# Attention inputs in a hybrid layer: q's heads transposed in pairs and split behind the transpose, k doubled ahead of one transpose, the row maximum negated, q's norm product on POOL

## The chip, the cores and the metric

The kernel runs on one core of a Trainium2 chip. The metric is the device time of one execution in microseconds (us). Before the change three runs gave a median of 1288.86 us (1288.18 to 1288.86). The engines are PE (TensorE: matrix products and transposes, results in PSUM), DVE (VectorE), ACT (ScalarE), POOL (GpSimd, which here works on SBUF alone) and SP (SyncE, which issues all DMAs).

## The reference

One layer on 2048 positions of width 1024. A normalised input goes through one projection; half of its columns feed a gated DeltaNet scanned in both directions (4 heads of 128), the other half a windowed attention (8 query heads, 2 key/value heads, width 64). Both results are gated, joined and projected back. The change touches the attention alone:

```python
q = rotary(rms_norm(q.reshape(b, s, 8, 64), q_norm_w), cos, sin)
k = rotary(rms_norm(k.reshape(b, s, 2, 64), k_norm_w), cos, sin)
...
scores = jnp.einsum('bnqhgd,bnkhd->bnhgqk', qb, kb) * (SWA_HEAD_DIM ** -0.5)
scores = jnp.where(valid[None, :, None, None], scores, -jnp.inf)
mx = jnp.maximum(jnp.max(scores, axis=-1, keepdims=True), sink)
p = jnp.exp(scores - mx)
denom = jnp.sum(p, axis=-1, keepdims=True) + jnp.exp(sink - mx)
out = jnp.einsum('bnhgqk,bnkhd->bnqhgd', p / denom, vb)
```

Blocks of 128 queries see 384 keys: their own block and one on each side.

## The kernel before

All data is f32. Matrix products that need the full precision are made from parts in a rounded format (`F32R`): a value is split into a high part (a rounding copy, on ACT) and a low part (the value less the high part, on DVE), and the products of the parts are added in PSUM.

**Stages.** `phase_a` goes over the sequence in two halves of 8 chunks of 128 positions. In a half it first projects keys, values and queries by position (`seq_chunk`, stored in DRAM), then goes over the chunks `c`: `kv_chunk` and `q_chunk` prepare keys and queries one chunk ahead, `attend` does the attention of the chunk before, and between them stand the projections by feature, which carry most of PE's work: `conv_pair` (the DeltaNet's q, k, v with their convolution; tiles `pf_c` on PE, four `acc` additions on DVE for each, L241) and `gate_pairs` (`pf_z`, nearly PE alone). In the first half two groups of gates are mixed in ahead of and behind the convolutions; in the second half only the convolutions are, and the gates follow after the attention. `phase_b` then does the DeltaNet's matrices, inverses and scans and the output projections.

**What the change touches.** `rope` (L272) rotates and normalises: POOL makes the rotated rows `t1` (L276 to L279), ACT and DVE the sums of squares `rs`, POOL the power -1/2 (L284), DVE the product of `t1` and `rs` (L285). `q_chunk` takes two groups of four heads: ACT copies the group to the high part of `qd`, DVE makes the low part beside it (L321, L322), so each head has 128 columns, its high and its low 64. PE transposes each head into a PSUM tile `ptq` (L326), and ACT copies the four to `q2` (L327), whose rows 0 to 63 are then the high part and 64 to 127 the low one. `kv_chunk` does the same for a key head with the high part doubled (`kd`, two copies of 64 columns) and the low part doubled: four transposes a chunk (L308) and a copy to `k2` (L309). In `attend` two products a head (L343, L344) give the scores; one DVE instruction (L345) adds the mask and takes the row maximum, starting from the head's sink; another (L349) negates the maximum into `nm`, which ACT's exponential takes as its bias (L350). POOL multiplies the probabilities `pr` by the reciprocal sum (L359), PE transposes them (L364, PSUM tiles `pt`), ACT and DVE split them (`ph`, `pl`), and PE multiplies with the values.

**Buffers.** `ptq`, `ptk` and `pt` share a ring of two PSUM tiles (pool `pst`); the scores have two tiles of their own, the projections three, the output one.

**Order.** The order on each engine is not the order of the code. `set_order` collects all instructions, their dependencies and the rings of buffers, and a list scheduler with a cost for each instruction writes an order for every engine, which then holds. So an edit at one place can move instructions anywhere in the program.

Of the kernel before, what the change touches and what calls it, by code (L numbers as in the profile page):

```python
# [10 lines left out]
ALU = mybir.AluOpType  # L11
# [56 lines left out]
def phase_a(ctx, wide, tc, t, ident, nw, bd, gp, mix_sw, kq_d, v_d, zdn_d, zsw_d, q_pool):  # L68
# [24 lines left out]
    for a, src in ((qw, t["qw"]), (kw, t["kw"])):  # L93
        dma(a[:, 0], src.partition_broadcast(P))
        dma(a[:, 1, 0:32], src[32:64].partition_broadcast(P))
        dma(a[:, 1, 32:64], src[0:32].partition_broadcast(P))
    sink = const("sink", [P, NQ], t["sinks"].partition_broadcast(P))
    edge = const("edge", [P, 12, 4])
    half_neg = const("half_neg", [P, 16])
    V.memset(half_neg, -0.5)  # L100
    A.activation(cw, cw, AF.Copy, scale=0.5)
    A.activation(qw, qw, AF.Copy, scale=0.125)

    xhi, xlo = {}, {}

# [166 lines left out]
    def rope(src, n, tab, name):  # L272
        sv = src.rearrange("p (h d) -> p h d", d=64)
        t1 = sp.tile([P, 8, 64], F32, tag="t1", name=f"t1{name}")[:, :n]
        t2 = sp.tile([P, 8, 64], F32, tag="t2", name=f"t2{name}")[:, :n]
        G.tensor_tensor(t1, sv, tab[:, 0:1].to_broadcast([P, n, 64]), ALU.mult)  # L276
        G.tensor_tensor(t2[:, :, 0:32], sv[:, :, 32:64], tab[:, 1:2, 0:32].to_broadcast([P, n, 32]), ALU.mult)
        G.tensor_tensor(t2[:, :, 32:64], sv[:, :, 0:32], tab[:, 1:2, 32:64].to_broadcast([P, n, 32]), ALU.mult)
        G.tensor_tensor(t1, t1, t2, ALU.add)  # L279
        rs = sp.tile([P, 8], F32, tag="rsq", name=f"rs{name}")[:, :n]  # L280
        A.activation(t2, sv, AF.Square)
        V.tensor_reduce(rs, t2, axis=AX.X, op=ALU.add)
        G.tensor_scalar(rs, rs, 1.0 / 64, EPS, ALU.mult, ALU.add)
        G.tensor_tensor(rs, rs, half_neg[:, :n], ALU.pow)  # L284
        V.tensor_tensor(t1, t1, rs.unsqueeze(2).to_broadcast([P, n, 64]), ALU.mult)  # L285
        return t1

    def kv_chunk(c):
        sl = c % 4 + 2
        if c and c % 4 == 0:  # L290
            V.tensor_copy(k2[:, :, :, 0 : 2 * P], k2[:, :, :, 4 * P : 6 * P].bitcast(F32))
            V.tensor_copy(v2[:, 0:2], v2[:, 4:6].bitcast(F32))
        kv = sp.tile([P, 2 * P], F32, tag="kv", name=f"kv{c}")
        dma(kv, kv_d[c])
        kk = kv[:, 0:P]
        vv = kv[:, P : 2 * P].rearrange("p (h d) -> p h d", d=64)
        A.activation(v2[:, sl, :, 0:64], vv, AF.Copy)
        G.tensor_tensor(v2[:, sl, :, 64:128], vv, v2[:, sl, :, 0:64].bitcast(F32), ALU.subtract)
        kn = rope(kk, 2, rope_tab(c, kw, "k"), f"k{c}")
        kd = sp.tile([P, 512], F32R, tag="qd", name=f"kd{c}")  # L300
        kd = kd.rearrange("p (g s a d) -> p g s a d", g=2, s=2, a=2)
        knb = kn.unsqueeze(2).to_broadcast([P, 2, 2, 64])
        A.activation(kd[:, :, 0], knb, AF.Copy)
        V.tensor_tensor(kd[:, :, 1], knb, kd[:, :, 0].bitcast(F32), ALU.subtract)
        pt = pst.tile([P, 4, P], F32, tag="pst", name=f"ptk{c}")
        for g in range(2):
            for s in range(2):
                T.transpose(pt[:, 2 * g + s], kd[:, g, s].rearrange("p a d -> p (a d)").bitcast(F32), ident)  # L308
        A.activation(k2[:, :, :, sl * P : (sl + 1) * P], pt.rearrange("p (g s) n -> p g s n", g=2), AF.Copy)  # L309

    def q_chunk(c):
        qq = sp.tile([P, 512], F32, tag="qq", name=f"ql{c}")
        dma(qq, q_d[c])
        tab = rope_tab(c, qw, "q")
        r = []
        qa = rope(qq, 8, tab, f"q{c}")
        for g in range(2):
            qn = qa[:, 4 * g : 4 * g + 4]
            qd = sp.tile([P, 512], F32R, tag="qd", name=f"qd{c}_{g}")
            qd = qd.rearrange("p (h a d) -> p h a d", h=4, a=2)  # L320
            A.activation(qd[:, :, 0], qn, AF.Copy)  # L321
            V.tensor_tensor(qd[:, :, 1], qn, qd[:, :, 0].bitcast(F32), ALU.subtract)  # L322
            q2 = sp.tile([P, 4, P], F32R, tag="q2", name=f"q2_{c}_{g}", bufs=4)
            pt = pst.tile([P, 4, P], F32, tag="pst", name=f"ptq{c}_{g}")
            for j in range(4):
                T.transpose(pt[:, j], qd[:, j].rearrange("p a d -> p (a d)").bitcast(F32), ident)  # L326
            A.activation(q2, pt, AF.Copy)  # L327
            r.append(q2)
        return r

    def attend(c, q2):
        sl = 1 if c % 4 == 3 and c < NCH - 1 else c % 4 + 2
        lo, hi = (1 if c == 0 else 0), (2 if c == NCH - 1 else 3)
        n = (hi - lo) * P
        k0 = (sl - 1 + lo) * P
        for g in range(2):
            pr = [sp.tile([P, 3 * P], F32, tag="pr", name=f"pr{c}_{g}_{j}", bufs=6) for j in range(4)]
            st = sp.tile([P, 4, 4], F32, tag="st", name=f"st{c}_{g}")
            mx, nm, den, es = (st[:, i] for i in range(4))
            for j in range(4):  # L340
                hh = 4 * g + j
                ps = pss.tile([P, 3 * P], F32, tag="pss", name=f"s{c}_{hh}")
                T.matmul(ps[:, :n], q2[g][:, j], k2[:, g, 0, k0 : k0 + n], start=True, stop=False)  # L343
                T.matmul(ps[:, :n], q2[g][:, j], k2[:, g, 1, k0 : k0 + n], start=False, stop=True)  # L344
                V.tensor_tensor_reduce(  # L345
                    pr[j][:, :n], ps[:, :n], mask[:, lo * P : hi * P], 1.0, sink[:, hh : hh + 1],
                    ALU.add, ALU.max, accum_out=mx[:, j : j + 1],
                )
                V.tensor_scalar(nm[:, j : j + 1], mx[:, j : j + 1], -1.0, None, ALU.mult)  # L349
                A.activation(  # L350
                    pr[j][:, :n], pr[j][:, :n], AF.Exp, bias=nm[:, j : j + 1], accum_out=den[:, j : j + 1]
                )
            V.tensor_tensor(es, sink[:, 4 * g : 4 * g + 4], mx, ALU.subtract)
            A.activation(es, es, AF.Exp)
            V.scalar_tensor_tensor(den, den, 1.0, es, ALU.mult, ALU.add)
            V.tensor_scalar(den, den, 2.0, None, ALU.mult)
            V.reciprocal(den, den)  # L357
            for j in range(4):
                G.tensor_scalar(pr[j][:, :n], pr[j][:, :n], den[:, j : j + 1], 1.0, ALU.mult, ALU.mult)  # L359
            po = pso.tile([P, 512], F32, tag="pso", name=f"po{c}_{g}")  # L360
            for kb in range(lo, hi):
                pt = pst.tile([P, 4, P], F32, tag="pst", name=f"pt{c}_{g}_{kb}")
                for j in range(4):
                    T.transpose(pt[:, j], pr[j][:, (kb - lo) * P : (kb - lo + 1) * P], ident)  # L364
                ph = sp.tile([P, 512], F32R, tag="ph", name=f"ph{c}_{g}_{kb}")
                pl = sp.tile([P, 512], F32R, tag="pl", name=f"pl{c}_{g}_{kb}")
                ptf = pt.rearrange("p a b -> p (a b)")
                A.activation(ph, ptf, AF.Copy)  # L368
                V.tensor_tensor(pl, ptf, ph.bitcast(F32), ALU.subtract)  # L369
                vk = v2[:, sl - 1 + kb, g]  # L370
                T.matmul(po, vk, ph, start=(kb == lo), stop=False)
                T.matmul(po, vk, pl, start=False, stop=(kb == hi - 1))
            ot = sp.tile([P, 2, P], F32, tag="ot", name=f"ot{c}_{g}")
            pv = po.rearrange("p (a b n) -> p a b n", a=2, b=2)
            A.activation(ot[0:64], pv[64:128, :, 0], AF.Copy)
            A.activation(ot[64:128], pv[64:128, :, 1], AF.Copy)
            V.tensor_tensor(ot[0:64], pv[0:64, :, 0], ot[0:64], ALU.add)
            V.tensor_tensor(ot[64:128], pv[0:64, :, 1], ot[64:128], ALU.add)
# [875 lines left out]
def layout(inputs):  # L1254
# [22 lines left out]
    cs = np.ascontiguousarray(cs.reshape(NCH, P, 2, 64).transpose(1, 0, 2, 3))  # L1277
    i, j = np.arange(P)[:, None], np.arange(P)[None, :]
    rel = np.arange(3 * P)[None, :] - P - i
    smask = np.where(np.abs(rel) <= 128, f(0), f(NEG)).astype(f)  # L1280
    le = (i <= j)
    tri = np.stack([le, ~le | (i == j), np.ones((P, P), bool)], 1).astype(f)
    dmask = np.stack([np.where(le, f(0), f(NEG)), np.where(i >= j, f(0), f(NEG))], 1).astype(f)
# [26 lines left out]
```

## Time and profile before

| | |
|---|---|
| median of 3 runs | 1288.86 us |
| the profiled execution's own time | 1286.12 us |
| its span in the trace | 1284.2 us |
| granted TensorE clock, mean | 0.993 |
| attention's score products (L343), first to last | 174.9 to 671.1 us |
| q's transposes (L326), first to last | 160.8 to 638.5 us |

The profile is one execution. A row of instructions gives line, engine, operation, the tiles written and read, the shapes and the count, then busy time and the mean of one in ns, then the idle time of the engine just before them and what ended it. A window's row gives its start and end, its length, the busy time (and count) of PE, weight load, DVE, ACT and POOL in it, the granted clock, the DMA share and GB/s. A row of waits gives who waited for whom, the total in us, how many times, the longest. A row of the chain gives start, length, engine and line of a piece of the work that ended last.

### The profile page before, as it was taken

What the parts mean: (1) busy time and instruction counts of PE and PEld (TensorE: products, weight loads), DVE (VectorE), ACT (ScalarE), POOL (GpSimd) and SP (SyncE); (2) the same over time, 40 slices, a digit from 0 to 9 for tenths busy, and PEclk for the clock granted to TensorE, in tenths of its full rate; (3) what the DMA queues carried; (4) which work ended last, traced back from release to release, by engine and by line L of the source; (5) the groups of instructions that cost most, each with busy time, mean ns of one, the idle gap of its engine ahead of it and who ended that gap; (6) DMA issues with size and microseconds to landing.
All of it is one profiled execution on the core that took longest, in us unless ns stands there. A gap on an engine that the chain in (4) does not pass through costs nothing.

```text
span 1284.2 us, 22568 instructions
## 1 busy us (share of the span) xinstructions
PE 1227.4 (96%) x7162; PEld 1056.0 (82%) x7162; DVE 901.8 (70%) x2266; ACT 718.8 (56%) x2121; POOL 507.8 (40%) x876
## 2 busy tenths in 40 slices
PE   6999999999999999999999998899799899999998
PEld 6998878788889987888888787788688789898776
DVE  4422488999874679999996583689489779557333
ACT  6421265776644677777665425858557855666210
POOL 2230054566512387774321306513681651641000
PEclk9999999999999999999999999999899999999999
DMA  7442254223544333421237816967965874746765
GB/s 259 150 127 79 97 169 158 88 83 101 177 130 131 121 106 111 124 98 50 75 115 242 237 63 196 283 192 206 278 172 157 242 202 139 207 148 201 242 233 210
DMA packets 225510, 205.35 MB, mean 160 GB/s; under 512 B 48496, under 2 KB 175088, under 8 KB 225392
## 3 DMA queue, kind: packets, MB, share of 16 engines
q1 hardware_dynamic: 225392, 203.92, 51.2%
q8 instruction: 57, 0.93, 0.3%
q14 instruction: 61, 0.50, 0.1%
HBM read 138.79 MB, written 65.08 MB: 159 GB/s over the span
## 4 chain that ended last, share of the span: by engine, by line
PE 67%; DVE 9%; DMA 9%; ACT 5%; POOL 4%; issue 4%; SPq 1%; DVEq 0%; POOLq 0%; ACTq 0%
PE pf_c L190 5%; PE pf_c L191 5%; PE pf_c L192 5%; PE pf_z L190 4%; PE pf_z L191 4%; PE pf_z L192 4%; PE pi L773 3%; PE pt L364 3%; PE pcd L562 2%; PE pcd L563 2%; PE pcd L564 2%; DVE acc L241 2%; PE pcs L601 2%; PE py L822 1%; PE pcs L600 1%
## 5 line engine op out<-in xcount | busy, mean ns | idle before, releaser
L190 PE MATMUL pf_c<-xhi,wh_c 128*128 128x512 f32 x384 | 151.3, 405 | 1.1 <-DVE acc L241 1.1
L191 PE MATMUL pf_c<-xlo,wh_c 128*128 128x512 f32 x384 | 152.0, 404 | 0.0
L192 PE MATMUL pf_c<-xhi,wl_c 128*128 128x512 f32 x384 | 150.6, 404 | 0.0
L241 DVE SCALAR_TENSOR_TENSOR acc<-pf_c,cw,acc 128x512 f32<-128x512 f32 (+1 forms) x192 | 140.4, 742 | 10.4 <-ACT acc L237 8.1
L359 POOL TENSOR_SCALAR pr<-pr,st 128x384 f32<-128x384 f32 (+1 forms) x128 | 88.8, 711 | 72.3 <-DVE st L357 56.5
L190 PE MATMUL pf_z<-xhi,wh_z 128*128 128x512 f32 x256 | 87.0, 403 | 0.5 <-DVE zo L214 0.5
L191 PE MATMUL pf_z<-xlo,wh_z 128*128 128x512 f32 x256 | 86.5, 399 | 0.0
L350 ACT ACTIVATE pr<-pr,st 128x384 f32<-128x384 f32 (+1 forms) x128 | 76.1, 597 | 17.7 <-DVE st L349 16.4
L192 PE MATMUL pf_z<-xhi,wl_z 128*128 128x512 f32 x256 | 85.3, 398 | 0.0
L190 PEld LDWEIGHTS pf_c<-xhi,wh_c 128*128 128x128 f32 x384 | 72.5, 189 | 14.8 <-DVE acc L241 1.5
L192 PEld LDWEIGHTS pf_c<-xhi,wl_c 128*128 128x128 f32 x384 | 72.2, 189 | 13.2
L191 PEld LDWEIGHTS pf_c<-xlo,wh_c 128*128 128x128 f32 x384 | 72.1, 189 | 13.1
L368 ACT ACTIVATE ph<-pt 128x512 fp32r<-128x512 f32 x92 | 53.8, 595 | 41.6 <-PE pt L364 38.2
L345 DVE CUSTOM_DVE_ANT_0 pr<-s,mask,sink 128x384 f32<-128x384 f32 (+1 forms) x128 | 73.0, 592 | 5.7 <-PE pt L364 3.2
L364 PE MATMUL pt<-ident,pr 128*128 128x128 f32 x368 | 72.1, 275 | 3.7 <-DVE pl L369 2.3
L369 DVE TENSOR_TENSOR pl<-pt,ph 128x512 fp32r<-128x512 f32 x92 | 62.0, 682 | 15.7 <-ACT ph L368 14.1
L827 ACT ACTIVATE yk<-py,ck 128x128 f32<-128x128 f32 x120 | 43.9, 366 | 44.6 <-PE py L822 43.3
L364 PEld LDWEIGHTS pt<-ident,pr 128*128 128x128 f32 x368 | 48.0, 140 | 20.2 <-DVE pl L369 4.3
L704 DVE SCALAR_TENSOR_TENSOR ma<-gh,bp,dc 128x256 f32<-128x256 f32 x128 | 54.6, 475 | 11.4 <-PE gh L695 7.6
L600 PE MATMUL pcs<-wohs,mhs 128*128 128x512 f32 x128 | 57.7, 451 | 5.0 <-ACT mhs L594 5.0
L201 PE MATMUL pq_q<-wh_q,xhi 128*128 128x256 f32 x256 | 60.6, 286 | 0.1
L202 PE MATMUL pq_q<-wh_q,xlo 128*128 128x256 f32 x256 | 60.0, 282 | 0.0
(253 smaller groups left out, 3743.7 us busy)
## 6 DMA issues: line engine op xcount, KB each, us to landing
kqc<-kq_d SPq DMA_DIRECT2D x120, 128.0 KB, 2.9
ws_c<-wt SPq DMA_DIRECT2D x48, 256.0 KB, 3.2
xr<-x SPq DMA_DIRECT2D x16, 512.0 KB, 5.5
ws_z<-wt SPq DMA_DIRECT2D x32, 256.0 KB, 3.7
kq<-kq_d SPq DMA_DIRECT2D x16, 512.0 KB, 5.1
m_d<-ma SPq DMA_DIRECT2D x32, 256.0 KB, 5.9
mxs<-mix_sw SPq DMA_DIRECT2D x32, 256.0 KB, 3.3
xrs<-x SPq DMA_DIRECT2D x32, 256.0 KB, 3.5
```

The lines of the kernel that those rows point to most:

```text
L190: T.matmul(ps, hi[:, k, cs], xhi[b][:, k], start=(k == 0), stop=False)
L191: T.matmul(ps, hi[:, k, cs], xlo[b][:, k], start=False, stop=False)
L192: T.matmul(ps, lo[:, k, cs], xhi[b][:, k], start=False, stop=(k == KC - 1))
L201: T.matmul(ps[:, :n], xh, hi[:, k, :n], start=(k == 0), stop=False)
L202: T.matmul(ps[:, :n], xl, hi[:, k, :n], start=False, stop=False)
L241: V.scalar_tensor_tensor(av, ps[:, lo:], cw[:, i, k : k + 1], av, ALU.mult, ALU.add)
L345: V.tensor_tensor_reduce(pr[j][:, :n], ps[:, :n], mask[:, lo * P : hi * P], 1.0, sink[:, hh : hh + 1], ALU.add, ALU.max, accum_out=mx[:, j ...
L350: A.activation(pr[j][:, :n], pr[j][:, :n], AF.Exp, bias=nm[:, j : j + 1], accum_out=den[:, j : j + 1])
L359: G.tensor_scalar(pr[j][:, :n], pr[j][:, :n], den[:, j : j + 1], 1.0, ALU.mult, ALU.mult)
L364: T.transpose(pt[:, j], pr[j][:, (kb - lo) * P : (kb - lo + 1) * P], ident)
L369: V.tensor_tensor(pl, ptf, ph.bitcast(F32), ALU.subtract)
L600: T.matmul(ps, mh[:, k], wh[:, k], start=(k == 0), stop=False)
```

## The change

In `q_chunk` two neighbouring heads (2 x 64 columns of the f32 rows) share one transpose, so a group takes two instead of four; the split into high and low part is made behind it, from PSUM: for each of the two halves of 64 rows ACT writes the high part to rows 0 to 63 of `q2`, and DVE the low part to rows 64 to 127. For the keys the product with `rs` writes each head's 64 columns twice (`kd`), one transpose a head follows, and high and low part are made from PSUM. The product of q's rows with `rs` goes from DVE to POOL. q's weight is negated, so the scores come out negative; mask and sink are negated too, the row instruction takes the minimum, which is the negated maximum as such, and the exponential multiplies its input by -1: L349 goes.

```diff
@@ const tables
+    G.tensor_scalar(sink, sink, -1.0, None, ALU.mult)
-    A.activation(qw, qw, AF.Copy, scale=0.125)
+    A.activation(qw, qw, AF.Copy, scale=-0.125)
@@ rope
-        V.tensor_tensor(t1, t1, rs.unsqueeze(2).to_broadcast([P, n, 64]), ALU.mult)
+        if n == 2:
+            kd = sp.tile([P, 2, 2, 64], F32, tag="kd", name=f"kd{name}")
+            rb = rs.unsqueeze(2).unsqueeze(3).to_broadcast([P, 2, 2, 64])
+            V.tensor_tensor(kd, t1.unsqueeze(2).to_broadcast([P, 2, 2, 64]), rb, ALU.mult)
+            return kd
+        G.tensor_tensor(t1, t1, rs.unsqueeze(2).to_broadcast([P, n, 64]), ALU.mult)
@@ kv_chunk
-        A.activation(kd[:, :, 0], knb, AF.Copy)
-        V.tensor_tensor(kd[:, :, 1], knb, kd[:, :, 0].bitcast(F32), ALU.subtract)
-        pt = pst.tile([P, 4, P], F32, tag="pst", name=f"ptk{c}")
+        pt = pst.tile([P, 4, P], F32, tag="pst", name=f"ptk{c}")[:, :2]
         for g in range(2):
-            for s in range(2):
-                T.transpose(pt[:, 2 * g + s], kd[:, g, s].rearrange("p a d -> p (a d)").bitcast(F32), ident)
-        A.activation(k2[:, :, :, sl * P : (sl + 1) * P], pt.rearrange("p (g s) n -> p g s n", g=2), AF.Copy)
+            T.transpose(pt[:, g], kn[:, g].rearrange("p a d -> p (a d)"), ident)
+        kc = slice(sl * P, (sl + 1) * P)
+        A.activation(k2[:, :, 0, kc], pt, AF.Copy)
+        V.tensor_tensor(k2[:, :, 1, kc], pt, k2[:, :, 0, kc].bitcast(F32), ALU.subtract)
@@ q_chunk
-            A.activation(qd[:, :, 0], qn, AF.Copy)
-            V.tensor_tensor(qd[:, :, 1], qn, qd[:, :, 0].bitcast(F32), ALU.subtract)
-            pt = pst.tile([P, 4, P], F32, tag="pst", name=f"ptq{c}_{g}")
-            for j in range(4):
-                T.transpose(pt[:, j], qd[:, j].rearrange("p a d -> p (a d)").bitcast(F32), ident)
-            A.activation(q2, pt, AF.Copy)
+            pt = pst.tile([P, 4, P], F32, tag="pst", name=f"ptq{c}_{g}")[:, :2]
+            for j in range(2):
+                T.transpose(pt[:, j], qn[:, 2 * j : 2 * j + 2].rearrange("p h d -> p (h d)"), ident)
+            for j in range(2):
+                A.activation(q2[0:64, j::2], pt[64 * j : 64 * j + 64], AF.Copy)
+                V.tensor_tensor(q2[64:128, j::2], pt[64 * j : 64 * j + 64], q2[0:64, j::2].bitcast(F32), ALU.subtract)
@@ attend
-                    ALU.add, ALU.max, accum_out=mx[:, j : j + 1],
+                    ALU.add, ALU.min, accum_out=nm[:, j : j + 1],
                 )
-                V.tensor_scalar(nm[:, j : j + 1], mx[:, j : j + 1], -1.0, None, ALU.mult)
                 A.activation(
-                    pr[j][:, :n], pr[j][:, :n], AF.Exp, bias=nm[:, j : j + 1], accum_out=den[:, j : j + 1]
+                    pr[j][:, :n], pr[j][:, :n], AF.Exp, bias=nm[:, j : j + 1], scale=-1.0, accum_out=den[:, j : j + 1]
                 )
-            V.tensor_tensor(es, sink[:, 4 * g : 4 * g + 4], mx, ALU.subtract)
+            V.tensor_tensor(es, nm, sink[:, 4 * g : 4 * g + 4], ALU.subtract)
@@ layout
-    smask = np.where(np.abs(rel) <= 128, f(0), f(NEG)).astype(f)
+    smask = np.where(np.abs(rel) <= 128, f(0), f(-NEG)).astype(f)
```

The scheduler writes a new order for the whole program. Three places of it follow, all at chunk 9, in the second half's attention. In a row stand line, operation, the tile written, the tiles read and the shape of the output; tiles carry running numbers at the end. Lines of the changed kernel differ by a few from those before.

On PE, q's transposes of chunk 9 among the projections; before:

```order
L326 MATMUL ptq_0_5569<-ident,qd_0_5565 128x128 x4
L191 MATMUL pf_c_1_0_5390<-xlo_4077,wh_c_1_5368 128x512
L192 MATMUL pf_c_1_0_5390<-xhi_4076,wl_c_1_5369 128x512
L190 MATMUL pf_c_1_0_5390<-xhi_4076,wh_c_1_5368 128x512
L191 MATMUL pf_c_1_0_5390<-xlo_4077,wh_c_1_5368 128x512
L192 MATMUL pf_c_1_0_5390<-xhi_4076,wl_c_1_5369 128x512
L190 MATMUL pf_c_1_0_5390<-xhi_4076,wh_c_1_5368 128x512
L326 MATMUL ptq_1_5579<-ident,qd_1_5575 128x128
L191 MATMUL pf_c_1_0_5390<-xlo_4077,wh_c_1_5368 128x512
L372 MATMUL po_1_5325<-pl_1_1_5343,v_148 128x512
L192 MATMUL pf_c_1_0_5390<-xhi_4076,wl_c_1_5369 128x512
L371 MATMUL po_1_5325<-ph_1_2_5353,v_148 128x512
```

and now:

```order
L324 MATMUL ptq_0_5434<-ident,t1q_5421 128x128 x2
L371 MATMUL po_1_5196<-pl_1_2_5225,v_149 128x512
L192 MATMUL pf_c_1_0_5261<-xlo_3966,wh_c_1_5239 128x512
L193 MATMUL pf_c_1_0_5261<-xhi_3965,wl_c_1_5240 128x512
L324 MATMUL ptq_1_5442<-ident,t1q_5421 128x128 x2
L191 MATMUL pf_c_1_0_5261<-xhi_3965,wh_c_1_5239 128x512
L343 MATMUL s_6_5538<-k_148,q_8_1_5077 128x384
L192 MATMUL pf_c_1_0_5261<-xlo_3966,wh_c_1_5239 128x512
L343 MATMUL s_7_5543<-k_148,q_8_1_5077 128x384
L344 MATMUL s_6_5538<-k_148,q_8_1_5077 128x384
L344 MATMUL s_7_5543<-k_148,q_8_1_5077 128x384
L194 MATMUL pf_c_1_0_5261<-xhi_3965,wl_c_1_5240 128x512
```

Each group has two transposes instead of four, read straight from the normalised rows `t1q`. Fourteen matmuls stand between the second group's transposes and the next tile of the `pst` ring (`pt` of head 0).

On ACT, the copies out of these tiles, with the waits that each row carries (the engine whose semaphore it waits for); before:

```order
L354 ACTIVATE st_0_5589<-st_0_5589 128x4 [waits DVE_49]
L327 ACTIVATE q_9_0_5568<-ptq_0_5569 128x512 [waits PE_49]
L281 ACTIVATE t2k_5900<-kv_5891 128x128 [waits Pool_49]
L281 ACTIVATE t2q_5927<-ql_5920 128x512 [waits DMAHW6_49,Pool_49]
L327 ACTIVATE q_9_1_5578<-ptq_1_5579 128x512 [waits PE_49]
```

and now:

```order
L326 ACTIVATE q_9_0_5433<-ptq_0_5434 64x2x128 [waits PE_49]
L374 ACTIVATE ot_1_5230<-po_1_5196 64x256 [waits DMAHW3_49,PE_49]
L349 ACTIVATE pr_1_0_5523,st_1_5527<-pr_1_0_5523,st_1_5527 128x384 [waits DVE_49]
L326 ACTIVATE q_9_1_5441<-ptq_1_5442 64x2x128 [waits PE_49]
L375 ACTIVATE ot_1_5230<-po_1_5196 64x256
L349 ACTIVATE pr_1_1_5524,st_1_5527<-pr_1_1_5524,st_1_5527 128x384 [waits DVE_49]
L326 ACTIVATE q_9_0_5433<-ptq_0_5434 64x2x128 [waits DVE_49]
L326 ACTIVATE q_9_1_5441<-ptq_1_5442 64x2x128 [waits DVE_49]
L182 ACTIVATE wh_c_1_5597<-ws_c_1_4_5607 128x2x256 [waits DMAHW4_49]
```

One copy of a tile has become two, and the second of each waits for DVE, which writes the other rows of the same tile between them.

On DVE, the row maximum of heads 2 and 3 of chunk 8; before:

```order
L345 ISA pr_0_2_5587,st_0_5589<-s_2_5602,mask,sink 128x384 [waits PE_49,Pool_49]
L345 ISA st_0_5589 128x1
L345 ISA pr_0_3_5588,st_0_5589<-s_3_5608,mask,sink 128x384 [waits PE_49,Pool_49]
L345 ISA st_0_5589 128x1
L349 TENSOR_SCALAR st_0_5589<-st_0_5589 128x1 [waits DVE_49]
L369 TENSOR_TENSOR pl_1_2_5354<-pt_1_2_5348,ph_1_2_5353 128x512 [waits PE_49,Activation_49]
L349 TENSOR_SCALAR st_0_5589<-st_0_5589 128x1 [waits DVE_49]
L353 TENSOR_TENSOR st_0_5589<-sink,st_0_5589 128x4
```

and now:

```order
L345 ISA pr_0_2_5451,st_0_5453<-s_2_5464,mask,sink 128x384 [waits PE_49,Pool_49]
L345 ISA st_0_5453 128x1
L345 ISA pr_0_3_5452,st_0_5453<-s_3_5469,mask,sink 128x384 [waits PE_49,Pool_49]
L345 ISA st_0_5453 128x1
L183 TENSOR_TENSOR wl_c_1_5598<-ws_c_1_0_5599,wh_c_1_5597 128x2x256 [waits DMAHW5_49,Activation_49]
L368 TENSOR_TENSOR pl_1_2_5225<-pt_1_2_5219,ph_1_2_5224 128x512 [waits PE_49,Activation_49]
L352 TENSOR_TENSOR st_0_5453<-st_0_5453,sink 128x4 [waits DVE_49]
```

The two negations (L349) are gone, and the exponentials follow on the row instruction itself; a split of the probabilities stood between the two negations.

More of the change, by code (lines that the diff above doesn't have):

```diff
@@ L299, in kv_chunk @@
         kn = rope(kk, 2, rope_tab(c, kw, "k"), f"k{c}")
[L300 to L304, printed above, removed]
-        pt = pst.tile([P, 4, P], F32, tag="pst", name=f"ptk{c}")
+        pt = pst.tile([P, 4, P], F32, tag="pst", name=f"ptk{c}")[:, :2]
         for g in range(2):
-            for s in range(2):
-                T.transpose(pt[:, 2 * g + s], kd[:, g, s].rearrange("p a d -> p (a d)").bitcast(F32), ident)
-        A.activation(k2[:, :, :, sl * P : (sl + 1) * P], pt.rearrange("p (g s) n -> p g s n", g=2), AF.Copy)
+            T.transpose(pt[:, g], kn[:, g].rearrange("p a d -> p (a d)"), ident)
+        kc = slice(sl * P, (sl + 1) * P)
+        A.activation(k2[:, :, 0, kc], pt, AF.Copy)
+        V.tensor_tensor(k2[:, :, 1, kc], pt, k2[:, :, 0, kc].bitcast(F32), ALU.subtract)
     def q_chunk(c):
@@ L318, in q_chunk @@
             qn = qa[:, 4 * g : 4 * g + 4]
[L319 to L322, printed above, removed]
             q2 = sp.tile([P, 4, P], F32R, tag="q2", name=f"q2_{c}_{g}", bufs=4)
-            pt = pst.tile([P, 4, P], F32, tag="pst", name=f"ptq{c}_{g}")
-            for j in range(4):
-                T.transpose(pt[:, j], qd[:, j].rearrange("p a d -> p (a d)").bitcast(F32), ident)
-            A.activation(q2, pt, AF.Copy)
+            pt = pst.tile([P, 4, P], F32, tag="pst", name=f"ptq{c}_{g}")[:, :2]
[4 more added lines that the diff above has]
+                V.tensor_tensor(q2[64:128, j::2], pt[64 * j : 64 * j + 64], q2[0:64, j::2].bitcast(F32), ALU.subtract)
             r.append(q2)
@@ L337, in attend @@
             pr = [sp.tile([P, 3 * P], F32, tag="pr", name=f"pr{c}_{g}_{j}", bufs=6) for j in range(4)]
-            st = sp.tile([P, 4, 4], F32, tag="st", name=f"st{c}_{g}")
-            mx, nm, den, es = (st[:, i] for i in range(4))
+            st = sp.tile([P, 3, 4], F32, tag="st", name=f"st{c}_{g}")
+            nm, den, es = (st[:, i] for i in range(3))
             for j in range(4):
```

## Prediction, before the changed kernel was run

> **What bounds the kernel now.** First the page's busy shares and its slices of the span, to find the bounding engine in each stage; all edits lie in the attention stage, so the slices there matter.
>
> ```profile
> span 1284.2 us, 22568 instructions
> PE 1227.4 (96%) x7162; PEld 1056.0 (82%) x7162; DVE 901.8 (70%) x2266; ACT 718.8 (56%) x2121; POOL 507.8 (40%) x876
> PE   6999999999999999999999998899799899999998
> DVE  4422488999874679999996583689489779557333
> ```
>
> A slice is 32 us. PE shows 9 everywhere in the first 700 us; DVE shows 8 and 9 in two stretches, which are the attention of the two halves of the sequence. Next the windows of these stretches, and who PE waits for between 160 and 680 us:
>
> ```profile
> 160.00:380.00 220.00, 218.20 (x1092) 179.32 (x1091) 192.64 (x447) 140.40 (x315) 116.17 (x170) 1.00 0.39 126
> 480.00:680.00 200.00, 196.98 (x1004) 161.50 (x1003) 192.76 (x471) 140.22 (x342) 104.66 (x148) 1.00 0.31 99
> PE pt L364 <- DVE pl L369: 2.3, 4, 0.9
> PE pt L364 <- POOL pr L359: 1.3, 3, 0.7
> ```
>
> The columns after the length are busy times of PE, weight load, DVE, ACT and POOL. In the first half PE has 218 of 220 us and DVE 193 (88%): PE bounds it, because the gate projections, almost pure PE work, are mixed in there. In the second half the gates come later, and DVE is busy 192.8 of 200 us beside PE's 197: two engines are full, and either may set the pace. ACT (70%) and POOL (52%) have room. PE's own waits are a few us in all; so work taken from PE is time, and work taken from DVE may be time in the second half.
>
> **PE: 96 transposes fewer.** Before, a chunk takes 8 transposes for q and 4 for k; now 4 and 2. Over 16 chunks 64 + 32 = 96 go, and nothing is added on PE.
>
> ```profile
> L326 PE MATMUL ptq<-ident,qd 128*128 128x128 f32 x128 | 20.5, 272 | 0.0
> L308 PE MATMUL ptk<-ident,kd 128*128 128x128 f32 x64 | 10.3, 274 | 0.3 <-DVE pl L369 0.3
> 585.06 0.87 PE ptq L326 x8
> ```
>
> One lasts 272 ns, but the chain of waits has eight in a row in 0.87 us, 0.109 us each: they overlap. I price them by the chain: 96 x 0.109 = 10.5 us, some 5.2 us in each half. Below that it can't go while PE bounds; the upper bound, by the duration, is 96 x 0.272 = 26.1 us.
>
> [...]
>
> **DVE: less, in the stage where it is full.**
>
> ```profile
> L322 DVE TENSOR_TENSOR qd<-t1q,qd 128x256 fp32r<-128x256 f32 x32 | 15.0, 476 | 0.6 <-ACT qd L321 0.5
> L304 DVE TENSOR_TENSOR kd<-t1k,kd 128x256 fp32r<-128x256 f32 x16 | 8.1, 503 | 1.9 <-ACT kd L303 1.9
> L285 DVE TENSOR_TENSOR t1q<-t1q,rsq 128x512 f32<-128x512 f32 x16 | 16.2, 1015 | 5.9 <-POOL rsq L284 3.7 <-POOL acc L231 2.1
> L285 DVE TENSOR_TENSOR t1k<-t1k,rsk 128x128 f32<-128x128 f32 x16 | 6.6, 415 | 2.5 <-POOL rsk L284 2.4
> L349 DVE TENSOR_SCALAR st<-st 128x1 f32<-128x1 f32 x128 | 16.1, 144 | 0.2
> L378 DVE TENSOR_TENSOR ot<-po,ot 64x256 f32<-64x256 f32 x32 | 13.4, 418 | 0.9
> L377 DVE TENSOR_TENSOR ot<-po,ot 64x256 f32<-64x256 f32 x32 | 13.1, 408 | 2.1 <-ACT ot L376 1.9
> L704 DVE SCALAR_TENSOR_TENSOR ma<-gh,bp,dc 128x256 f32<-128x256 f32 x128 | 54.6, 475 | 11.4 <-PE gh L695 7.6 <-PE po L840 2.5 <-ACT dc L703 0.7
> ```
>
> Removed: the first five rows, 15.0 + 8.1 + 16.2 + 6.6 + 16.1 = 62.0 us. Added: 64 subtractions of 64x256 from PSUM for q, the very form of L377 and L378, 64 x 0.413 = 26.4 us; 16 of 128x256 from PSUM for k, between 0.41 (L377) and 0.475 (L704), taken as 0.44: 7.0 us; 16 doubled products of 128x256 with both inputs in SBUF, by L304's 0.503: 8.0 us. Together 41.4, so DVE loses 20.6 us, 10.3 in each half. In the first half that is hidden behind PE and worth nothing more. In the second half it is worth at most 10.3 us (DVE alone paces) and at least PE's 5.2. Both engines stand within 4 us of full there, and the row maximum's negation was a link between DVE and ACT in every head, so I take 8.3, nearer DVE's end.
>
> [...]
>
> ```profile
> L285 DVE TENSOR_TENSOR t1q<-t1q,rsq x16: 673/890/1803, 92.6 to 631.6; 128x512 f32<-128x512 f32 x16
> ```
>
> At its shortest the removed product would be 16 x 0.673 = 10.8 us instead of 16.2, and DVE's relief 15.2.
>
> **ACT.** 32 copies of 128x256 and of 128x512 for q, and 16 of each for k, become 64 of 64x256 and 16 of 128x256 from PSUM.
>
> ```profile
> L321 ACT ACTIVATE qd<-t1q 128x256 fp32r<-128x256 f32 x32 | 12.9, 414 | 7.6 <-DVE t1q L285 4.4 <-PE ptk L308 2.7
> L327 ACT ACTIVATE q<-ptq 128x512 fp32r<-128x512 f32 x32 | 18.7, 594 | 4.7 <-PE ptq L326 4.2
> L303 ACT ACTIVATE kd<-t1k 128x256 fp32r<-128x256 f32 x16 | 6.7, 417 | 10.1 <-DVE t1k L285 10.1
> L309 ACT ACTIVATE k<-ptk 128x512 fp32r<-128x512 f32 x16 | 9.4, 587 | 0.9 <-PE ptk L308 0.8
> L375 ACT ACTIVATE ot<-po 64x256 f32<-64x256 f32 x32 | 12.2, 381 | 26.2 <-PE po L372 25.9
> L260 ACT ACTIVATE sgq<-pq_q 128x256 f32<-128x256 f32 x32 | 11.2, 377 | 15.2 <-PE pq_q L203 13.0 <-issue 1.4 <-DMA kv_d<-sgkv 0.7
> ```
>
> Removed 47.7 us, added 64 x 0.381 + 16 x 0.377 = 30.4: 17.3 less on an engine with room, counted as nothing. The exponential's scale of -1 is an immediate; no row prices it, and between 0 and a few ns for 128 instructions I take 0.
>
> **POOL: more.** The q product moves here:
>
> ```profile
> L279 POOL TENSOR_TENSOR t1q<-t1q,t2q 128x512 f32<-128x512 f32 x16 | 22.1, 1381 | 0.4
> L666 POOL TENSOR_TENSOR dc<-dc,dmask 128x512 f32<-128x512 f32 x24 | 31.0, 1297 | 19.5 <-DMA dc<-gr_d 19.2
> ```
>
> 16 x 1.30 to 1.38, so 22 us more, 11 in a half: in the second window POOL goes from 105 to some 115 of 200 us. The cover is its idle time; behind the product on the queue stand the next normalisations of `pr` (L359), which PE's transposes wait for. The sign change of `sink` is one small instruction at the start, 0. No DMA is added or moved by the edit itself.
>
> **The new waits.** A q tile's PSUM buffer (`pst`, two of them, shared with the probabilities' transposes) was freed by one copy of 0.594 us. Now ACT, DVE, ACT and DVE follow each other, since the second ACT copy waits for DVE in the order shown above: 0.38 + 0.41 + 0.38 + 0.41 = 1.58 us and what DVE's queue adds. Behind the ACT copy stand exponentials and weight copies. In the rows of chunk 9 PE has fourteen matmuls between the q transposes and the next user of the ring, so I count 0; the other bound is in the rival.
>
> **Sum.** 5.2 + 8.3 = 13.5 us off the profiled execution of 1286.1 us (span 1284.2): 1272.6. The median of the runs is 2.7 above that execution, so 1275.4 for the median. The later stages do nothing new, but are ordered anew; their chain has pieces such as
>
> ```profile
> 826.36 6.03 DMA mxs<-mix_sw
> 1105.81 5.74 DMA zcs<-zsw_d
> ```
>
> One such piece won or lost is 6 us either way, with no reason for a sign: 1269 to 1281 around the forecast.
>
> **Rivals.** (a) DVE sets the pace in both halves: -20.6, 1268. For it: the slices with 9 on DVE in the first half too; against: 88% there. (b) Transposes cost their whole duration: -26, 1263; the chain's row is against it. [...] (c) POOL's product comes ahead of `pr` on the way that PE waits for: 16 x 1.38 = 22 us if each is exposed; half of them exposed give back 11 us, 1286. For it: PE already waited for POOL `pr`; against: only 1.3 us in all. (d) The new order costs two pieces of 6 us in the later stages: 1288. (e) Slower: the ring of two `pst` tiles. If PE stands for the longer hold, 32 tiles x (1.58 - 0.59) = 32 us and DVE's queue on top, 1307; it decides against the gain from 13.5 / 32 = 0.42 us a tile. For it: DVE is full, so each of the handoffs can wait; against: PE's order has other work in between.
>
> **How the numbers follow.** Forecast 0.62, (a) 0.15, (b) 0.03, (c) 0.06, (d) 0.06, (e) 0.08. About 0.2% (2.6 us) is what a measurement of this kernel can tell from no change, so faster means below 1286.3 and slower above 1291.4. Faster: forecast, (a), (b) and half of (c), 0.83; same: half of (c) and most of (d), 0.07; slower: (e) and the rest of (d), 0.10. The range goes from 1264, under (a) by a part of a DMA piece, to 1288, up to (c) and (d); outside lie (b), (e) and the outer halves of (c) and (d), under 0.2.
>
> **What would show it.** PE: 96 rows fewer at 0.109 us, the attention's last transposes some 13 us earlier. DVE's windows of the second half below 90% with PE at 99%: then DVE's relief was real; if DVE is still at 96% and PE's idle unchanged, it paced and (a) is nearer. PE waiting for DVE's or ACT's `q` rows would show (e); PE waiting more for POOL `pr` (c). An attention stage shorter by 13 us with an unchanged end would show (d). The prediction is wrong if the attention stage does not get shorter at all.

## The result: about 11 us faster

The changed kernel takes 1277.67 us (median of 8 runs, 1274.25 to 1285.01), the kernel before in the same series 1288.52 us (1287.14 to 1294.34). The ratio is 0.9914, with a 95% interval from 0.9893 to 0.9935: 11 us less, give or take 3. The forecast was 1275.4.

The profiled execution took 1274.25 us, the fastest of the eight and 3.4 us under their median, with a span of 1272.5; that of before, 1286.12 us, lies 2.4 under its median, with a span of 1284.2. The busy shares and the slices of the profile after (columns as before):

```profile
span 1272.5 us, 22253 instructions
PE 1219.4 (96%) x7066; PEld 1044.4 (82%) x7066; DVE 889.5 (70%) x2154; ACT 703.2 (55%) x2105; POOL 507.4 (40%) x893
PE   6999999999999999999999998998799899999998
DVE  4422387999975589999986573788488879557333
```

PE has 96 instructions fewer and 8.0 us less of busy time. DVE's busy time, in which instructions that overlap count once, fell by 12.3 us. Where in the span the time went is read from first and last starts. Each row gives count, shortest, median and longest duration in ns, then the first and the last start; the last key projection (`pq_kv`) closes the first half, the last convolution product (`pf_c`) the second. Before:

```profile
L201 PE MATMUL pq_kv<-wh_kv,xhi x128: 282/288/596, 9.8 to 419.8; 128*128 128x272 f32 x128
L190 PE MATMUL pf_c<-xhi,wh_c x384: 387/394/508, 129.1 to 681.3; 128*128 128x512 f32 x192
```

After:

```profile
L202 PE MATMUL pq_kv<-wh_kv,xhi x128: 282/288/595, 10.0 to 416.9; 128*128 128x272 f32 x128
L191 PE MATMUL pf_c<-xhi,wh_c x384: 387/394/501, 127.5 to 671.2; 128*128 128x512 f32 x192
```

The first half ends 2.9 us earlier (416.9 against 419.8). The second half takes 671.2 - 416.9 = 254.3 us instead of 681.3 - 419.8 = 261.5: 7.2 us less. The span ends 11.7 us earlier, so the later stages gave 1.6 us more. Some 60% of the gain lies in the stage where the prediction put the larger part. The windows of the two stretches after:

```profile
160.00:380.00 220.00, 216.45 (x1057) 176.13 (x1056) 191.80 (x406) 134.02 (x311) 115.00 (x177) 1.00 0.40 128
480.00:680.00 200.00, 198.96 (x986) 160.11 (x985) 189.17 (x421) 135.66 (x337) 103.15 (x145) 1.00 0.36 112
```

In the second stretch PE went from 197 to 199 of 200 us, and DVE from 193 to 189; but the last 9 us of this window now lie behind the second half. Over the second half as it is measured above, before and after:

```profile
419.80:681.30 261.50, 257.47 (x1445) 218.04 (x1444) 236.19 (x599) 182.45 (x449) 144.20 (x204) 1.00 0.32 103
416.90:671.20 254.30, 253.12 (x1396) 211.55 (x1395) 228.44 (x535) 175.59 (x443) 145.81 (x212) 1.00 0.35 106
```

PE nearly filled this half before and fills it now; DVE's share stayed at 90%. Of the 7.2 us, 4.3 are busy time of PE and 2.9 are time in which PE stood idle. And the instructions that the prediction priced, by shapes:

```profile
L324 PE MATMUL ptq<-ident,t1q 128*128 128x128 f32 x64 | 12.0, 275 | 0.1
L308 PE MATMUL ptk<-ident,kdk 128*128 128x128 f32 x32 | 6.4, 272 | 0.0
L327 DVE TENSOR_TENSOR q<-ptq,q 64x256 fp32r<-64x256 f32 x64 | 26.6, 422 | 6.6 <-ACT q L326 4.7
L311 DVE TENSOR_TENSOR k<-ptk,k 128x256 fp32r<-128x256 f32 x16 | 6.6, 414 | 0.1
L289 DVE TENSOR_TENSOR kdk<-t1k,rsk 128x256 f32<-128x256 f32 x16 | 10.8, 678 | 10.9 <-POOL rsk L285 10.9
L326 ACT ACTIVATE q<-ptq 64x256 fp32r<-64x256 f32 x64 | 23.6, 376 | 14.5 <-PE ptq L324 7.5 <-DVE q L327 6.2
L291 POOL TENSOR_TENSOR t1q<-t1q,rsq 128x512 f32<-128x512 f32 x16 | 16.9, 1057 | 0.4
```

Most came as estimated: 0.422 us for 0.413, 0.414 for 0.44, 0.376 for 0.38. The doubled key product took 0.678 instead of 0.503, POOL's product 1.06 instead of 1.30 to 1.38. By groups DVE lost the 62.0 us of the prediction's rows and got 26.6 + 6.6 + 10.8 = 44.0: 18 us of relief where 20.6 were counted. ACT waited 6.2 us in all for DVE between the copies of a tile.

### The profile page after: what moved, and what is told of

Same layout as the page of the kernel before. It is cut to its first block, busy times and chain, and to the rows that moved or that the text cites. A ratio compares the mean times of both kernels' runs of the same rounds, so it can differ in the third digit from the quotient of the medians.

```text
span 1272.5 us, 22253 instructions
## 1 busy us (share of the span) xinstructions
PE 1219.4 (96%) x7066; PEld 1044.4 (82%) x7066; DVE 889.5 (70%) x2154; ACT 703.2 (55%) x2105; POOL 507.4 (40%) x893
## 4 chain that ended last, share of the span: by engine, by line
PE 67%; DVE 12%; DMA 9%; ACT 7%; issue 3%; POOL 1%; SPq 0%; DVEq 0%; ACTq 0%; POOLq 0%
PE pf_c L191 4%; PE pf_c L192 4%; PE pf_c L193 4%; PE pf_z L191 4%; PE pf_z L192 4%; PE pf_z L193 4%; PE pi L772 4%; DVE acc L242 3%; PE pt L363 3%; PE pq_q L202 2%; PE pq_q L204 2%; PE pq_q L203 2%; PE pcd L561 2%; PE pcd L563 2%; PE pcd L562 2%
## 5 line engine op out<-in xcount | busy, mean ns | idle before, releaser
L358 POOL TENSOR_SCALAR pr<-pr,st 128x384 f32<-128x384 f32 (+1 forms) x128 | 80.1, 648 | 71.3 <-DVE st L356 60.0
L349 ACT ACTIVATE pr<-pr,st 128x384 f32<-128x384 f32 (+1 forms) x128 | 76.1, 596 | 19.6 <-DVE st L345 19.1
L363 PE MATMUL pt<-ident,pr 128*128 128x128 f32 x368 | 67.2, 274 | 1.9 <-DVE q L327 1.1
L703 DVE SCALAR_TENSOR_TENSOR ma<-gh,bp,dc 128x256 f32<-128x256 f32 x128 | 54.9, 476 | 10.4 <-PE gh L694 8.7
L814 DVE SCALAR_TENSOR_TENSOR r<-pk,negc,vs 128x128 f32<-128x128 f32 x120 | 41.5, 346 | 27.1 <-PE pk L812 26.6
```

What stands on the lines that cost most here:

```text
L349: A.activation(pr[j][:, :n], pr[j][:, :n], AF.Exp, bias=nm[:, j : j + 1], scale=-1.0, accum_out=den[:, j : j + 1])
L703: V.scalar_tensor_tensor(ma[d, c4][:, c], gh[:, k], bp[:, d, cc : cc + 1], gms[d][:, c : c + 1].to_broadcast([P, 2, P]), ALU.mult, ALU.mult,)
```

## The experiments

Three stages are followed through all runs: the first half (start to the last key projection), the second (to the last convolution product) and the rest (to the last output product), each from the profiled execution. That is one execution of a kernel; it lies between 3.4 us under the kernel's median (the changed kernel) and 3.3 above it, so the differences of the stages need not add up to that of the medians. The lines below give the edit; the table behind them has all times.

**The transposes put back.** In the changed kernel each transpose is issued twice; the double lands in the half of the tile that nobody reads.

```diff
             T.transpose(pt[:, g], kn[:, g].rearrange("p a d -> p (a d)"), ident)
+            T.transpose(pt4[:, 2 + g], kn[:, g].rearrange("p a d -> p (a d)"), ident)
...
                 T.transpose(pt[:, j], qn[:, 2 * j : 2 * j + 2].rearrange("p h d -> p (h d)"), ident)
+                T.transpose(pt4[:, 2 + j], qn[:, 2 * j : 2 * j + 2].rearrange("p h d -> p (h d)"), ident)
```

> The changed kernel with the 96 transposes put back as doubles into the unused half of the same PSUM tile (results not read); DVE, ACT and POOL keep the changed work. Theory PE (the gain is the 96 transposes at 0.109 us on a PE that paces the attention): 10.5 us of PE work return, so the time goes back to within 2 us of the kernel before, 1286 to 1289. Theory DVE (the gain is DVE's relief): DVE's work is as in the changed kernel, so the time stays within 3 us of its 1277.7.

1290.66 us, ratio to before 1.0023 (1.0006 to 1.0040). In this order the 96 instructions cost the whole gain and a little more than theory PE gave, with DVE's relief left in. Both halves got longer than in the changed kernel, by 7.0 and 8.7 us. The second took 263.0 us, more than before (261.5) though DVE has 21 us less to do in the whole kernel, so here DVE's relief does not show.

**The row maximum alone**, in the kernel before (the hunks of `attend`, the sink, q's weight and the mask).

> The kernel before with the negated row maximum alone: 128 DVE instructions of 0.144 us fewer (16.1 us, more than three quarters of DVE's whole relief), PE unchanged. Theory PE: within 2 us of before, 1286 to 1290. Theory DVE: the second half gets shorter by up to 8 us, 1280 to 1283.

1287.64 us, ratio 0.9994 (0.9971 to 1.0017). The total did not change, as theory PE has it, but the second half went from 261.5 to 256.5, as theory DVE asks, and the first from 419.8 to 426.8. Part of that is one wait at the start of the attention, where PE waited 3.3 us for DVE's `acc` (1.1 before); in the 20 us that hold this wait the granted clock was 0.83 (180 to 200 us), and 1.00 in the 20 us before and behind:

```profile
PE pf_c L191 <- DVE acc L242: 3.3, 1, 3.3
```

So the total alone would have hidden what happened in the second half.

**q's norm product back on DVE**, in the changed kernel.

```diff
-        G.tensor_tensor(t1, t1, rs.unsqueeze(2).to_broadcast([P, n, 64]), ALU.mult)
+        V.tensor_tensor(t1, t1, rs.unsqueeze(2).to_broadcast([P, n, 64]), ALU.mult)
```

> The changed kernel with q's norm product on DVE again, as before: 16 instructions, 11 to 16 us back on DVE, 17 us off POOL, PE unchanged. Theory PE: within 2 us of the changed kernel, 1276 to 1280. Theory DVE: 5 to 8 us longer, 1283 to 1286. A rival on POOL (its product delays the normalisation of pr): shorter than the changed kernel by 2 us or more.

1294.71 us, 17 us above the changed kernel and above the one before (ratio 1.0057, 1.0036 to 1.0078): more than any theory gave. The second half is 6.0 us longer, as theory DVE has it. The first is 7.8 us longer, and holds one long wait of PE:

```profile
PE s L343 <- ACT th L248: 7.7, 1, 7.7
```

**The q slots apart**, in the changed kernel.

```diff
-                A.activation(q2[0:64, j::2], pt[64 * j : 64 * j + 64], AF.Copy)
+                sj = slice(2 * j, 2 * j + 2)
+                A.activation(q2[0:64, sj], pt[64 * j : 64 * j + 64], AF.Copy)
```

(and the subtraction and the two score products with the same slots.)

> The changed kernel with q2's slots in another order (heads 0, 2, 1, 3), so that the two ACT copies of a tile write separate ranges and the second need not wait for DVE; no instruction more or less. If the chain ACT, DVE, ACT, DVE on the pst ring costs anything, up to 0.2 us a tile on 32 tiles: 1271 to 1275. If PE has other work in the meantime, as the prediction counted: 1276 to 1280.

1281.38 us, ratio 0.9948 (0.9933 to 0.9963). Not shorter: the second half took 255.0 for 254.3, and the loss is in the later stages, which the edit doesn't touch. The chain of four handoffs costs nothing that can be seen, as the prediction counted, though the time lies 1.4 us above what was expected for that case. But 4 us from work that is the same is a warning, and the next runs ask how much the order alone does.

**The small instructions back**, in the changed kernel, writing a column that nobody reads.

```diff
+                V.tensor_scalar(xt4[:, j : j + 1], nm[:, j : j + 1], -1.0, None, ALU.mult)
                 A.activation(
```

> The changed kernel with 128 DVE instructions of the form of the removed negation (128x1, 0.144 us) put back after the row instruction, writing a column that nobody reads: 16.1 us back on DVE, 8 us in each half; PE, ACT and POOL as in the changed kernel. Theory PE: within 2 us of the changed kernel's 1277.7. Theory DVE: 5 to 8 us longer. The row maximum alone shortened the second half (last key projection to last convolution product) by 5.0 us in its profile, so I expect the second half 4 to 6 us longer than the changed kernel's 254.3.

1288.09 us, ratio 0.9996 (0.9984 to 1.0009): 10.4 us above the changed kernel, more than the 5 to 8 of theory DVE. The second half took 260.5, 6.2 us more; the first half 3.2 more, the rest 6.6 more. These sum to 16: the two profiled executions lie on opposite sides of their medians.

**q's norm product on POOL alone**, in the kernel before (`G` for `V` where n is 8).

> The kernel before with q's norm product on POOL alone: DVE loses 16 us, POOL gains 17, PE unchanged. If both engines set the pace in the second half, that half gets 4 to 6 us shorter than 261.5 and the time is 1283 to 1286; theory PE alone: 1287 to 1291; if POOL delays pr: longer than 1291.

1283.28 us, ratio 0.9954 (0.9936 to 0.9972). The second half took 258.0, 3.5 us less, where 4 to 6 were expected. PE's waits for POOL's `pr` there are 1.6 us, about those of before (1.3).

**The same work in another order.** One number of the scheduler's model, in the changed kernel and in the one before:

```diff
-LAG = {"PE": 205, "DVE": 140, "Activation": 160, "Pool": 120, "SP": 2400}
+LAG = {"PE": 206, "DVE": 140, "Activation": 160, "Pool": 120, "SP": 2400}
```

> The changed kernel, instruction for instruction, with one number of the scheduler (the lag that it assumes after PE) moved from 205 to 206 ns: the order changes, the work does not. If what differs between kernels is their work, within 2 us of 1277.7; if the order alone moves the time, it shows by how much: I expect up to 5 us either way, most of it in the first half and in the later stages.

> The kernel before with the same number of the scheduler moved: the work of before in another order. Up to 5 us either way of 1289; the second half (last key projection to last convolution product) within 2 us of its 261.5 if that stage goes by the work of PE and DVE.

1280.74 us for the changed work and 1285.12 for that of before (ratios 0.9937, 0.9918 to 0.9957, and 0.9967, 0.9952 to 0.9982). The gap shrinks from 11 to 4 us. So a second pair was run, with 204:

> The changed kernel once more with the scheduler's lag after PE moved, to 204 ns: same work, third order. The first two orders took 1277.7 and 1280.7; between 1274 and 1284, second half between 254 and 259.

> The kernel before with the lag at 204 ns: same work, third order. The first two took 1288.9 and 1285.1; between 1283 and 1292, second half between 260 and 263. If the work makes the difference, its time lies above all three orders of the changed kernel.

1288.72 us for the changed work, 1288.41 for that of before: no gap at all. Both expectations missed: the changed work was to take 1274 to 1284, and the work of before was to lie above all three orders of the changed work. Three orders of before lie within 4 us; those of the changed work lie 11 us apart. In the slow one the PE waits of the first half hold the same wait as the run with the norm on DVE:

```profile
PE s L343 <- ACT th L248: 8.0, 1, 8.0
```

The chain of waits of that kernel around it (start, length, engine and line):

```profile
207.22 0.69 PE pf_c L191 x3
207.92 0.69 PE pf_c L192 x3
208.61 0.69 PE pf_c L193 x3
210.36 6.68 DVE acc L242 x10
217.11 1.06 ACT th L248
218.23 0.55 PE s L343
```

and the windows of the stretch (PE, weight load, DVE, ACT and POOL busy, then the granted clock):

```profile
198.00:209.00 11.00, 11.00 (x49) 8.93 (x48) 2.36 (x4) 0.36 (x1) 0.00 (x0) 1.00 0.20 71
209.00:218.00 9.00, 1.20 (x10) 0.91 (x8) 8.25 (x13) 5.39 (x11) 3.30 (x7) 0.74 0.45 131
218.20:223.20 5.00, 4.97 (x14) 4.13 (x15) 4.88 (x15) 4.05 (x13) 0.96 (x2) 0.50 0.27 108
```

This order lets PE run three convolution products interleaved, so that all three end together at 209; DVE, ACT and POOL have next to nothing to do for 11 us (2.4, 0.4 and 0). Then DVE has ten additions in a row, and PE waits 8 us for them. When it goes on, its clock is at 0.50. No instruction is added or taken away here; it is where the scheduler's list happened to put three tiles.

**The transposes' part alone**: pairs, doubled keys and splits from PSUM, with negation and norm on DVE as before.

> The kernel before with the transposes' part alone: pairs for q, doubled keys, splits from PSUM; the negation and q's norm product stay on DVE as before. PE loses 10.5 us, DVE gains 41.4 - 29.7 = 12 us, ACT loses 17. Theory PE alone: 10 us shorter than before, 1277 to 1280. Theory both engines pace the second half: PE's relief and DVE's burden cancel, 1287 to 1292, second half within 2 us of 261.9.

1301.81 us, ratio 1.0103 (1.0086 to 1.0120): 12 us slower than before with 96 transposes fewer. Theory PE is off by more than 20 us, and the theory that PE's relief and DVE's burden cancel (1287 to 1292) by 10: the second half took 269.5, 8 us above before. By their rows DVE's new instructions cost 12.2 us more than those they replace, as counted. The windows show an idle PE:

```profile
160.00:380.00 220.00, 212.34 (x1004) 168.15 (x1003) 195.66 (x450) 126.76 (x296) 109.84 (x169) 0.99 0.39 124
480.00:680.00 200.00, 189.98 (x929) 148.46 (x928) 189.82 (x479) 130.91 (x336) 101.80 (x146) 1.00 0.27 87
```

PE falls to 190 of 200 us, and DVE is the first among those it waits for between 160 and 680 us:

```profile
PE pf_c L190 <- DVE acc L241: 6.3, 9, 1.8
PE pt L363 <- POOL pr L358: 3.1, 8, 0.7
PE pf_z L190 <- DVE acc L241: 2.2, 1, 2.2
PE pt L363 <- DVE q L326: 1.8, 4, 0.5
```

**More off DVE**, in the changed kernel: the keys' doubled product on POOL, and the sum's factor 2 folded into the sink term.

```diff
-            V.tensor_tensor(kd, t1.unsqueeze(2).to_broadcast([P, 2, 2, 64]), rb, ALU.mult)
+            G.tensor_tensor(kd, t1.unsqueeze(2).to_broadcast([P, 2, 2, 64]), rb, ALU.mult)
...
+    sink2 = const("sink2", [P, NQ])
+    G.tensor_scalar(sink2, sink, -0.6931471805599453, None, ALU.add)
...
-            V.tensor_tensor(es, nm, sink[:, 4 * g : 4 * g + 4], ALU.subtract)
+            V.tensor_tensor(es, nm, sink2[:, 4 * g : 4 * g + 4], ALU.subtract)
...
-            V.scalar_tensor_tensor(den, den, 1.0, es, ALU.mult, ALU.add)
-            V.tensor_scalar(den, den, 2.0, None, ALU.mult)
+            V.scalar_tensor_tensor(den, den, 2.0, es, ALU.mult, ALU.add)
```

> The changed kernel with more taken from DVE: the keys' doubled product on POOL (16 instructions of 0.68 us) and the doubling of the sum folded into the sink term (32 of 0.24 us), 18.6 us in all; POOL gains 16 of some 0.85 us. PE unchanged. Theory both: the second half 3 to 5 us shorter than 254.8 unless PE is full there already, the time 1271 to 1277. Theory PE alone: 1276 to 1281.

1285.13 us, ratio 0.9953 (0.9935 to 0.9972): 7.5 us slower than the changed kernel, though with less work on DVE; the second half took 259.3. The expectation missed. Its first half holds a wait of PE of 3.1 us for `acc` at the start of the attention; the granted clock of the whole profiled execution was 0.989, for 0.992 in the changed kernel. With one order alone, the loss can't be told from the spread of the orders, and it is left open. No version here beats the changed kernel.

All of them together; stages from the profiled execution, times as medians. The column behind the second half splits it into PE's busy and idle time:

| kernel | PE, DVE work against before, us | first | second | PE busy + idle in it | rest | time |
|---|---|---|---|---|---|---|
| before | 0, 0 | 419.8 | 261.5 | 257.5 + 4.0 | 598.4 | 1288.5 |
| before, 206 | 0, 0 | 422.9 | 260.3 | 257.2 + 3.1 | 594.1 | 1285.1 |
| before, 204 | 0, 0 | 424.5 | 259.5 | 256.8 + 2.8 | 601.4 | 1288.4 |
| changed | -10.5, -21 | 416.9 | 254.3 | 253.1 + 1.2 | 596.8 | 1277.7 |
| changed, 206 | -10.5, -21 | 420.6 | 258.0 | 253.0 + 5.0 | 594.0 | 1280.7 |
| changed, 204 | -10.5, -21 | 426.6 | 258.6 | 253.6 + 5.1 | 599.6 | 1288.7 |
| changed, slots apart | -10.5, -21 | 418.1 | 255.0 | 253.5 + 1.5 | 602.9 | 1281.4 |
| changed, more off DVE | -10.5, -39 | 423.2 | 259.3 | 254.1 + 5.3 | 597.1 | 1285.1 |
| transposes put back | 0, -21 | 423.9 | 263.0 | 259.1 + 3.9 | 597.3 | 1290.7 |
| norm back on DVE | -10.5, -4 | 424.7 | 260.3 | 254.1 + 6.2 | 602.1 | 1294.7 |
| small instructions back | -10.5, -5 | 420.1 | 260.5 | 255.0 + 5.5 | 603.4 | 1288.1 |
| transposes' part alone | -10.5, +12 | 426.8 | 269.5 | 258.3 + 11.2 | 600.3 | 1301.8 |
| row maximum alone | 0, -16 | 426.8 | 256.5 | 255.8 + 0.7 | 598.7 | 1287.6 |
| norm on POOL alone | 0, -16 | 420.1 | 258.0 | 256.4 + 1.6 | 598.4 | 1283.3 |

The work column is the prediction's estimate from rows of before. PE's busy time is not its work alone: with the same matmuls it varies (253.1 in the changed kernel, 258.3 in the transposes' part alone).

## Why the prediction was right, and where it was not

**PE's transposes are time: borne out in direction, at a lower price.** PE's busy time fell by 8.0 us, 0.083 us for each of the 96, where 0.109 and 10.5 us in all were counted. In the second half PE is busy 256.8 to 257.5 us in the three orders of before and 253.0 to 253.6 in the three of the changed work: some 4 us in every order, for the 5.2 counted. Putting the transposes back cost 13 us in one order. With orders 11 us apart that gives no price, but its second half lies above every order of the changed work. The 26 us of rival (b) showed nowhere. By themselves, however, the transposes gave nothing; see below.

**DVE in the second half: the direction was right, the size was not shown.** Forecast 8.3 us, measured 7.2, but in one order. Two edits that touch no PE work brought that half to 256.5 and 258.0, under all three orders of before (259.5 to 261.5). Two that put DVE work back brought it to 260.3 and 260.5, 6 us above the changed kernel, but less than 2 above the highest of its other orders (258.6). So DVE's work can move the stage, and so can PE's, as the prediction's "either may set the pace" says; the run with the transposes put back does not fit, and that is open. On average over its orders the whole change brings 3.5 us there (257.0 over 254.3, 258.0 and 258.6, against 260.4 for before), less than the 5.2 that the prediction took as the least.

The step behind this is the bound "at most 10.3 us (DVE alone paces)" and the reason "both engines stand within 4 us of full". By the prediction's own row PE lacked 3 us of full and DVE 7. In the whole half PE stood idle for 4.0 us, so beside PE's own work DVE's relief could bring about those 4.0 us at most. (The row maximum alone brought 5.0, of which 3.3 were idle time; PE's busy time varies too.) The changed kernel got 2.9 of them in its order. In the two other orders PE's idle time was 5.0 and 5.1, more than before: the new splits also give PE something to wait for (1.7 us on DVE's `q` in the order of 206).

**The first half was mis-sized.** The forecast counted PE's 5.2 us there, and "that is hidden behind PE and worth nothing more" for DVE. Measured were 2.9 us, and 1.0 on average over the orders (421.4 against 422.4). In the changed kernel PE's busy time fell by 4.2 us from 10 us to the end of the half (403.1 to 399.0), and its idle time rose by 1.3. Whether DVE's work is hidden there is not shown: with 8 us of small instructions back this half took 420.1 us, and with the transposes' part alone, some 16 us more on DVE than in the changed kernel, 426.8. Both are about what the same work takes in other orders (416.9 to 426.6), and the row maximum alone, with less on DVE, took 426.8 too. One thing that differs between the orders is PE's wait for the convolutions' additions at the start of the attention: 0.4 us in the changed kernel, 1.2 and 10.4 in its other orders, 1.1 in before, 3.6 and 2.7 in its other orders.

**The step that was too narrow: "the later stages do nothing new, but are ordered anew ... 6 us either way".** The sum gave this spread to the later stages alone, where the changed kernel indeed won only 1.6 us. The orders moved the first half more: 416.9, 420.6 and 426.6 us for the same work. Over three orders each, the changed work takes 1282.4 us on average (1277.7, 1280.7, 1288.7) and that of before 1287.3 (1288.5, 1285.1, 1288.4). By these six kernels about 5 of the 11 us belong to the work and about 6 to the order that it happened to get. With orders 11 us apart that split is rough, and even the 5 us are not clear of nothing. The forecast of 13.5 us for the work looks too high by these averages, and the order made up for much of it: that the total came within 2.3 us of the forecast was in part luck. (Rival (d) is 1275.4 + 12 = 1287.4 by its own terms, not 1288; nothing hangs on it.)

**The signs.** The last of q's transposes starts 14.5 us earlier (624.0 for 638.5), where some 13 were expected. DVE's window of the second half was to fall below 90% if its relief was real, and to stay at 96% with PE's idle time unchanged if it paced alone. It came to 94.6% with PE at 99.5%, between the two.

**ACT and POOL.** Both counted as nothing. The exponential took as long with its factor of -1 as without (610 and 611 ns for the 128x384 form). The prediction had POOL 22 us busier; its busy time did not rise (507.8 and 507.4 us), because the product took 16.9 us and the 112 large normalisations of `pr` fell from 80.1 to 70.4 (732 and 652 ns each). With the transposes' part alone, they took 633 ns, so that part alone is enough for it; why was not tried. POOL's `pr` made PE wait 0.2 us between 160 and 680, less than the 1.3 before: rival (c) did not happen. **The ring of two tiles** cost PE 1.1 us of waits on DVE's `q` (rows below, PE's waits in that stretch after), and the run with separate slots won nothing: rival (e) did not happen.

```profile
PE pt L363 <- DVE q L327: 1.1, 2, 0.8
PE po L370 <- ACT ph L367: 1.0, 1, 1.0
PE pt L363 <- POOL pr L358: 0.2, 1, 0.2
```

**What the prediction did not ask** is what the change would be without its other parts. Moving the split behind the transpose costs DVE 12 us in stages where DVE is near full, and alone it made the kernel 12 us slower, though it takes the same work from PE. The gain came only together with the negation and the product on POOL, which take DVE work away. The run of the transposes' part is a single order too, but its second half (269.5) lies 8 us above all orders of before.

## What to carry to other kernels

Where two engines are both at 90% or more in a stage, as PE (98%) and DVE (90%) were in the second half here, price an edit on each of them, and take the idle time of the fuller one, here PE's 4.0 us, as about the most that relief of the other can bring (an estimate: the row maximum alone brought 5.0 us, 3.3 of them idle time): work taken off one and put on the other can lose, as 10.5 us off PE against 12 us on DVE did here. Where a scheduler writes the order, run the same work in two or three orders before a few microseconds are put down to an edit; here the orders of one and the same work lay up to 11 us apart. Read stages beside totals: the row maximum alone left the total unchanged, while its second half was 3 to 5 us shorter than in all orders of before.

## What the runs showed of the hardware

A wait of PE of 8 us cost more than itself. In the kernel with the order of 204, the granted clock behind it was 0.50 between 218.2 and 223.2 us (the windows above), and the same product went from 0.23 us to 0.43 us from start to start. The rows of PE's timeline (start, busy time, engine, line) ahead of the wait and behind it:

```profile
206.14 0.39 PE L193 MATMUL pf_c<-xhi,wl_c 128*128 128x512 f32 x1
206.37 0.39 PE L191 MATMUL pf_c<-xhi,wh_c 128*128 128x512 f32 x1
...
218.23 0.55 PE L343 MATMUL s<-k,q 128*128 128x256 f32 x1 [8.04 <-ACT th L248]
...
220.07 0.63 PE L193 MATMUL pf_c<-xhi,wl_c 128*128 128x512 f32 x1
220.50 0.63 PE L191 MATMUL pf_c<-xhi,wh_c 128*128 128x512 f32 x1
```

With 5 us at half rate it lost some 2.5 us more, an estimate from these rows. For this wait the trace shows 8 us of idle PE, then 5 us at 0.50, then full clock (1.00 between 224 and 236 us). Shorter waits came with a lower clock too. In the run with the row maximum alone PE waited 3.3 us, and the clock was 0.83 in the 20 us that hold the wait (180 to 200 us); in the run with the transposes put back it waited 2.6 us, and the clock was 0.91 between 180 and 200 us. In both runs it was 1.00 in the 20 us before and in the 20 us behind. In the changed kernel the longest wait of PE in the attention is 1.0 us, and its windows there (160 to 380 and 480 to 680 us) have a clock of 1.00.
